# Two-layer streaming encoder on one core: where the RWKV outputs of a pair of heads stand in PE's order, and the shape of the sample's output product

## The chip, the cores and the metric

The kernel runs on one core of a Trainium2 chip. The metric is the device time of one launch in microseconds. In what follows PE is TensorE (the matrix engine), ACT is ScalarE, VectorE is also shown as DVE, POOL is GpSimd and SP is the engine that issues the DMAs.

## The reference, cut to what matters

The model takes 512 prompt rows and 32 sample rows of width 1024 through two layers. Layer 0 is RWKV-7 time mixing over 24 heads of width 64, with memory attention and a gate; layer 1 is differential attention. The change concerns layer 0's recurrence:

```
def step(S, inp):
    r_t, k_t, v_t, w_t, kk_t, a_t = inp
    sa = jnp.einsum('bhvk,bhk->bhv', S, -kk_t)
    S = (S * w_t[:, :, None, :] + sa[..., None] * (kk_t * a_t)[:, :, None, :]
         + v_t[..., None] * k_t[:, :, None, :])
    return S, jnp.einsum('bhvk,bhk->bhv', S, r_t)
...
S_T, y = lax.scan(step, S0.astype(f32), xs)
```

The kernel doesn't run this row by row. It takes 64 rows as a chunk, and computes within the chunk with matrix products.

## The kernel before, in words

**Pairs and chunks.** The 24 heads go in 12 pairs; two heads of 64 fill the 128 partitions. A pair has 8 prompt chunks, one after the other since each needs the state of the one before, and one sample chunk (index 8) with a state of its own.

**A chunk** (`chunk`) has three steps. First `ps_c<-SB,zr` multiplies by the state, and VectorE adds the result to the values (`avz`). Then `ps_c<-avz,at` solves within the chunk, and ACT copies the result into the values' rows (`sv`). Then `ps_c<-sv,bt` gives the new state, which VectorE scales and adds (`SB`). For the sample the same tiles are called `ssi`, `ats`, `svs`, `bts`.

**Values and outputs.** `rw_values` makes the parts of the values that don't need the state: 16 products of 64x64 with 64 rows (`ps_v<-sv,at`, tile form 64\*64), copied by ACT to `avz`; the larger part of them, 14, is done in one step. `rw_outputs` multiplies the finished chunks by `at` for the output rows: 16 products of 64 columns with 128 rows (`ps_yc<-sv,at`, form 128\*64), added to `yt` by VectorE; its second step transposes the pair's final state and sends it out (`ps_so`). The sample's outputs are two such products (`ps_c<-svs,ats`), one for each head, made inside `chunk` with c == 8. In the profile an fp32 product counts as two PE instructions, so 16 products are a row with x32.

**Fills.** The projections (input columns for later pairs, gates, queries) are a stream of 128x272 products, `ps_g<-hh,whi`, `hl,whi`, `hh,wlo`, cut into single PE instructions, 192 for a pair that has four blocks. They are the bulk of PE's work, and they also fill the time in which a chunk waits for VectorE or ACT. I call one of them a fill. Their weights are split into a high and a low half by ACT (`whi`) and VectorE (`wlo`); this and the finishing of a projection (`raw`, `shc`, `rkv` on ACT, `rkv` on VectorE) is put off and taken up at free places by `some`.

**What sets the order.** Each engine's order is the order in which the program is written out; the five queues are tied. In a pair's loop over the 23 steps of `PLAN`, each step runs one step of the chain (`go("chain", pr)`), then the side work that the table names, first half and second half, then fills. A row's entries are (kind, distance of the pair, PE microseconds, VectorE microseconds). The sum of the PE numbers and the fills gives the pair's whole time; each step has a share of it (`due`), and gets fills until that share is used up:

```
while left and t + MAIN / 2 < (due[k + 1] if half else (due[k] + due[k + 1]) / 2):
    next(main)
    t += MAIN
    left -= 1
```

Side work that fills its step's share thus leaves no fills there. `prep` (a generator, `rw_prep`) prepares a later pair, `val` makes values, `smp` steps the sample, `out` makes outputs, `fin` normalises them, `mrg` joins parts of an inversion that POOL runs. `MPLAN` places the steps of the memory attention in pairs 10 and 11. After pair 11, `go("out", 11)` takes the next step of its outputs, and `TAIL` has one more `out`.

In a pair's second step, `prep` needs one of the projections finished: `r = rkv["r"]()`, and `decayed` makes `zr` from it on VectorE.

Of the kernel before, what the change touches and what calls it, by code (L numbers as in the profile page):

```python
# [14 lines left out]
ALU = mybir.AluOpType  # L15
# [30 lines left out]
LATER = 0.75  # L46
FULL = ("full", 0, 0, 0)
PLAN = [
    [[("val", 0, 0.95, 0), ("prep", 2, 0.1, 0)], [("prep", 2, 0, 0.42)]],
    [[], [("prep", 2, 0, 1.04)]],  # L50
    [[("prep", 1, 0.53, 0)], [("prep", 1, 0, 0), ("prep", 2, 0.56, 1.0)]],
    [[("prep", 2, 0, 0)], [("prep", 2, 0, 1.0)]],
# [3 lines left out]
    [[("prep", 2, 1.1, 1.37)], []],  # L56
    [[("smp", 0, 0.21, 0)], [("prep", 2, 0, 0.9)]],
    [[("prep", 2, 1.1, 1.37)], [("back", 1, 0, 0)]],
    [[("smp", 0, 0.6, 0.85)], []],
    [[("prep", 2, 0.5, 0.58)], [("at", 1, 0, 0), ("fin", -1, 0, 1.0)]],  # L60
    [[("prep", 2, 0.36, 0.43)], [("inv", 2, 0, 0), ("fin", -1, 0, 0.84)]],
    [[("prep", 2, 0.36, 0.43)], [("fin", -1, 0, 0), ("prep", 3, 0, 0)]],
# [5 lines left out]
    [[("prep", 3, 0.33, 0)], [("prep", 3, 0, 0.1), ("fin", -1, 0.6, 1.0)]],  # L68
    [[("prep", 3, 0.33, 0)], [("mrg", 1, 0.9, 0), ("prep", 3, 0.33, 0), ("fin", -1, 0, 0.73)]],
    [[("prep", 3, 0, 1.45), ("val", 1, 0.45, 0)], [("prep", 3, 0, 0.5)]],  # L70
    [[("out", 0, 1.6, 0.7)], [("prep", 3, 0, 0)]]]
MEMPE = 4.8
SHIFTED, KEPT = 13, 24
LAM = 5
# [2 lines left out]
MPLAN = {10: [(0, 0), (2, 0), (3, 0), (4, 0), (5, 0), (6, 0), (6.5, 1), (7, 0), (8, 0), (9, 0), (10, 0), (11, 0), (11.5, 0), (12.5, 1),  # L77
# [3 lines left out]

FILL0 = [4, 4, 8, 2, 6, 2, 2, 2, 6, 2, 18, 4, 4, 2, 2, 0, 8, 12, 4, 8, 14, 10, 6, 14, 2, 0, 2, 2, 2, 2, 2, 2]
FILL1 = [6, 14, 12, 2, 4, 2, 2, 2, 8, 0, 10, 0, 2, 8, 8, 6, 4, 6, 6, 8, 18, 12, 8, 10, 0, 0, 0, 0, 4]
# [24 lines left out]
class Trunk:  # L108
# [796 lines left out]
    H = [slice(0, 64), slice(64, P)]  # L905
# [33 lines left out]
    def chunk(self, st, c, S, Snew):  # L939

        nc, H, yt = self.nc, self.H, st["yt"]
        e, zs, ro, A, cv, cb = self.place(st, c)
        i = c // 2
        yield
        ps = self.psc.tile([P, 4, P], F32, tag="c", name="ps_c")
        rhs = self.avz[:, e, i, :]
        sd = None
        if c:
            self.te.matmul(ps[:, 0, :], st["zr"][:, c * P : c * P + P], S[:], start=True, stop=True)
            self.ve.tensor_tensor(rhs[zs], ps[zs, 0, :], rhs[zs], ALU.add)  # L950
            yield

        self.te.matmul(ps[:, 1, :], A[0].rearrange("p h t -> p (h t)"), rhs, start=True, stop=True)
        for h in range(2):
            self.ae.copy(cv[zs, H[h]], ps[H[h], 1, H[h]])
        if c:
            self.ae.copy(yt[ro, i, :], ps[ro, 0, :])
            sd = self.rb2.tile([P, P], F32, tag="sd", name="sd", bufs=RB)
            self.ae.activation(sd[:], S[:], AF.Copy, scale=st["dl"][:, c : c + 1])
        yield  # L960
        self.te.matmul(ps[:, 2, :], cb, cv, start=True, stop=True)
        if c == 8:
            self.outputs(st, (c,), ps, 3)
        for hc in H:
            d = st["dl"][hc, c : c + 1]
            if c == 0:
                self.ve.tensor_scalar(Snew[hc, hc], ps[hc, 2, hc], d, None, ALU.mult)
            else:
                self.ve.scalar_tensor_tensor(Snew[hc, hc], ps[hc, 2, hc], d, sd[hc, hc], ALU.mult, ALU.add)
        if c == 8:  # L970
            self.ve.tensor_tensor(yt[:64, 4, :], ps[:64, 3, :], yt[:64, 4, :], ALU.add)

    def rw_chain(self, st):

# [1254 lines left out]
```

## Time and profile before

| | |
|---|---|
| runs, median (all) | 1404.84 us (1404.56, 1404.84, 1409.58) |
| profiled execution | 1403.86 us, span 1401.70 us, granted clock 0.996 |
| PE busy | 1366.8 us, 98% |
| VectorE busy | 932.2 us, 67% |
| ACT busy | 825.4 us, 59% |
| POOL busy | 376.2 us, 27% |
| layer 0's pairs | from about 132 to 690 us, 46 us for each of pairs 1 to 8 |

Rows of the timeline give the start, the duration, the engine, the operation with its tiles, and in brackets the idle time before it with what ended it. PE's ends overlap, so its rows are read by their starts. L105 is the line of the helper through which all engines' instructions go.

### The profile page before, as it was taken

Reading aid. Unit: us, or ns where it says so; the run is one execution under the profiler, and the core shown is the slowest. Engines: PE = TensorE matmul, PEld = TensorE weight load, DVE = VectorE, ACT = ScalarE, POOL = GpSimd, SP = SyncE. Lnnn points to the kernel's source line nnn. Section 1 sums busy time; section 2 is a strip of 40 time slices with the busy share of each in tenths; the row PEclk is TensorE's granted clock in tenths of the full one; section 3 lists DMA queues with packets and bytes.
Section 4 is the critical chain, followed back from the end, with each engine's and each line's share of the span. In section 5 each row is a group of like instructions: output and inputs, shape, how many; then the busy total and the mean of one; then the engine's idle time right before and its main releaser. Section 6 shows DMA issues by size and latency. Waiting matters only on the chain.

```text
span 1401.7 us, 31899 instructions
## 1 busy us (share of the span) xinstructions
PE 1366.8 (98%) x11881; PEld 1304.5 (93%) x11881; DVE 932.2 (67%) x2345; ACT 825.4 (59%) x2292; POOL 376.2 (27%) x840
## 2 busy tenths in 40 slices
PE   8999999999999999999999999999999999999997
PEld 6998899999999998898899999999999999999997
DVE  5676777787877787666753476666467756767443
ACT  5765677767776777565543366664466546665222
POOL 2136568555865586520000040000000001001100
PEclk9999999999999999999999999999999999999999
DMA  7543222332233223342364474333333322332321
GB/s 224 155 119 83 61 54 64 84 86 71 69 81 97 61 64 82 81 136 71 114 201 125 124 211 114 92 91 87 107 92 92 104 75 84 94 107 86 91 76 72
DMA packets 264036, 139.45 MB, mean 99 GB/s; under 512 B 57721, under 2 KB 252802, under 8 KB 263882
## 3 DMA queue, kind: packets, MB, share of 16 engines
q1 hardware_dynamic: 263818, 137.41, 34.9%
q8 instruction: 94, 1.54, 0.5%
q14 instruction: 60, 0.49, 0.1%
q10 hardware_dynamic: 64, 0.02, 0.0%
HBM read 111.12 MB, written 22.91 MB: 96 GB/s over the span
## 4 chain that ended last, share of the span: by engine, by line
PE 83%; DVE 8%; ACT 4%; DMA 2%; issue 2%; SPq 1%; DVEq 0%; ACTq 0%
PE ps_g L105 58%; PE ps_c L105 5%; PE ps_s L105 2%; PE ps_o L105 2%; PE ps_at L105 2%; DVE wlo L105 2%; PE ps_v L105 1%; PE ps_mo L105 1%; SPq L105 1%; PE ps_mm L105 1%; PE ps_aT L105 1%; PE ps_w L105 1%; PE ps_yc L105 1%; PE ps_ss L105 1%; PE ps_kv L105 1%
## 5 line engine op out<-in xcount | busy, mean ns | idle before, releaser
L105 PE MATMUL ps_g<-hh,wlo 128*128 128x272 f32 x1808 | 537.8, 298 | 2.4 <-DVE wlo L105 2.4
L105 PE MATMUL ps_g<-hh,whi 128*128 128x272 f32 x1808 | 538.3, 298 | 0.4 <-DVE memk L105 0.2
L105 PE MATMUL ps_g<-hl,whi 128*128 128x272 f32 x1808 | 531.9, 295 | 0.6 <-DVE hl L105 0.3
L105 PEld LDWEIGHTS ps_g<-hh,wlo 128*128 128x128 f32 x1808 | 340.9, 189 | 7.9 <-DVE wlo L105 3.5
L105 PEld LDWEIGHTS ps_g<-hh,whi 128*128 128x128 f32 x1808 | 341.7, 189 | 5.1 <-DVE og L105 0.6
L105 PEld LDWEIGHTS ps_g<-hl,whi 128*128 128x128 f32 x1808 | 341.4, 189 | 4.6 <-DVE hl L105 1.2
L105 DVE TENSOR_TENSOR wlo<-raw,whi 128x512 fp32r<-128x512 f32 x314 | 220.0, 712 | 116.8 <-ACT whi L105 112.9
L105 ACT CAST whi<-raw 128x512 fp32r<-128x512 f32 x314 | 188.8, 618 | 108.4 <-PE ps_g L105 61.3
L853 POOL TENSOR_TENSOR tm<-u,m 102x84 f32<-102x84 f32 (+23 forms) x341 | 147.9, 434 | 165.5 <-DMA m<-sc 139.7
L855 POOL TENSOR_TENSOR u<-u,tm 102x84 f32<-102x84 f32 (+23 forms) x341 | 148.9, 437 | 26.7
L105 PE MATMUL ps_g<-hi,whi 128*128 128x272 f32 x512 | 148.9, 291 | 0.0
L105 PE MATMUL ps_g<-hi,wlo 128*128 128x272 f32 x512 | 147.7, 288 | 0.5 <-DVE wlo L105 0.5
L105 PE MATMUL ps_g<-lo,whi 128*128 128x272 f32 x512 | 147.4, 288 | 0.0
L1325 POOL TENSOR_TENSOR lo<-og,hi 128x544 fp32r<-128x544 f32 x8 | 13.2, 1652 | 359.5 <-ACT hi L105 359.1
L105 PEld LDWEIGHTS ps_g<-hi,wlo 128*128 128x128 f32 x512 | 96.4, 188 | 0.7 <-DVE wlo L105 0.7
L105 PEld LDWEIGHTS ps_g<-hi,whi 128*128 128x128 f32 x512 | 96.5, 188 | 0.0
L105 PEld LDWEIGHTS ps_g<-lo,whi 128*128 128x128 f32 x512 | 96.5, 188 | 0.0
L105 DVE SCALAR_TENSOR_TENSOR SB<-ps_c,dl,sd 64x64 f32<-64x64 f32 x168 | 47.5, 283 | 43.6 <-PE ps_c L105 37.2
L105 ACT ACTIVATE pt<-ps_s,snm 128x128 f32<-128x128 f32 (+3 forms) x96 | 50.9, 531 | 41.7 <-DVE snm L105 41.6
L1746 POOL TENSOR_TENSOR hl<-hn,hh 128x544 fp32r<-128x544 f32 x8 | 12.4, 1564 | 209.8 <-ACT hh L105 209.7
L105 ACT COPY sv<-ps_c 64x64 f32<-64x64 f32 x192 | 39.3, 205 | 44.3 <-PE ps_c L105 42.6
L105 ACT ACTIVATE sg<-ps_g 128x272 f32<-128x272 f32 x64 | 25.3, 395 | 56.1 <-PE ps_g L105 51.6
(399 smaller groups left out, 2586.8 us busy)
## 6 DMA issues: line engine op xcount, KB each, us to landing
raw<-in_rw_in_dram SPq DMA_DIRECT2D x114, 256.0 KB
raw<-in_df_in_dram SPq DMA_DIRECT2D x112, 256.0 KB
raw<-in_w_out_dram SPq DMA_DIRECT2D x64, 256.0 KB
oscr<-sg SPq DMA_DIRECT2D x16, 272.0 KB
lo<-oscr SPq DMA_DIRECT2D x16, 272.0 KB
m<-sc SPq DMA_DIRECT2D x33, 128.0 KB
raw<-in_w_mem_v_dram SPq DMA_DIRECT2D x16, 256.0 KB
kh<-kh SPq DMA_DIRECT2D x24, 136.0 KB
```

The source lines that it names most:

```text
L105: return lambda *a, **k: self.trunk.tie(self, issue(*a, **k))
L853: nc.gpsimd.tensor_tensor(tm[:, :n, :wd], u3[:, :n, kx : kx + 1].to_broadcast(sh), m3[:, kx : kx + 1, kx + 1 :].to_broadcast(sh), ALU.mult)
L855: nc.gpsimd.tensor_tensor(u3[:, :n, kx + 1 :], u3[:, :n, kx + 1 :], tm[:, :n, :wd], ALU.add)
L1325: (self.nc.gpsimd if g % 2 and self.o1 else self.ve).tensor_tensor(lo[:], t, hi[:].bitcast(F32), ALU.subtract)
L1746: nc.gpsimd.tensor_tensor(self.hl[:, k, :], h[:], self.hh[:, k, :].bitcast(F32), ALU.subtract)
```

## The change: what it does

The outputs of a pair move from the last step of its own loop to the first step of the next pair's loop, directly ahead of the large step of that pair's values. Their PE number becomes 1.1 instead of 1.6. The sample's outputs become one product of the whole 128x128 array, of which the two 64x64 diagonal blocks are used, each added to `yt` by an instruction of its own; the sample's PE number there becomes 0.44 instead of 0.6. In `MPLAN`, the steps of head 3 in pair 11 move back by one place from the second on.

```
 PLAN = [
-    [[("val", 0, 0.95, 0), ("prep", 2, 0.1, 0)], [("prep", 2, 0, 0.42)]],
+    [[("out", -1, 1.1, 0.6), ("val", 0, 0.95, 0), ("prep", 2, 0.1, 0)], [("prep", 2, 0, 0.42)]],
...
-    [[("smp", 0, 0.6, 0.85)], []],
+    [[("smp", 0, 0.44, 0.95)], []],
...
-    [[("out", 0, 1.6, 0.7)], [("prep", 3, 0, 0)]]]
+    [[], [("prep", 3, 0, 0)]]]
...
-              (11, 3), (12, 3), (13, 3), (14, 3), (15, 3), (16, 3), (17, 3), (18, 3), (19, 3)]}
+              (12.5, 3), (13, 3), (14, 3), (15, 3), (16, 3), (17, 3), (18, 3), (19, 3), (20, 3)]}
...
         if c == 8:
-            self.outputs(st, (c,), ps, 3)
+            self.te.matmul(ps[:, 3, :], A[1].rearrange("p h t -> p (h t)"), cv, start=True, stop=True)
...
         if c == 8:
-            self.ve.tensor_tensor(yt[:64, 4, :], ps[:64, 3, :], yt[:64, 4, :], ALU.add)
+            for hc in H:
+                self.ve.tensor_tensor(yt[:64, 4, hc], ps[hc, 3, hc], yt[:64, 4, hc], ALU.add)
```

How the instructions stand now. First PE at the boundary between pairs 5 and 6. `ps_yc` are pair 5's outputs, `ps_v` with a number pair 6's values, the first `ps_c<-sv,bt` is the last product of pair 5's chain and `ps_c<-avz` the first of pair 6's. Before:

```order
L105 MATMUL ps_g<-hl,whi 128x272
L105 MATMUL ps_c<-sv,bt 128x128
L105 MATMUL ps_yc<-sv,at_1686 64x64 x16
L105 MATMUL ps_g<-hh,wlo 128x272
L105 MATMUL ps_c<-avz,at_89 128x128
L105 MATMUL ps_v_6352<-sv,at_89 64x64
L105 MATMUL ps_v_6353<-sv,at_89 64x64
```

And now:

```order
L105 MATMUL ps_g<-hl,whi 128x272
L105 MATMUL ps_g<-hh,wlo 128x272
L105 MATMUL ps_c<-avz,at_89 128x128
L105 MATMUL ps_yc<-sv,at_1686 64x64 x16
L105 MATMUL ps_v_6352<-sv,at_89 64x64
L105 MATMUL ps_v_6353<-sv,at_89 64x64
```

The outputs have moved behind the first product of the next chain, next to the values; 13 fills, of which the last two are shown, now stand between `ps_c<-sv,bt` and `ps_c<-avz`, where there was one.

Next the same place a little later, from the last two values on. `ps_rt` is a transpose of the preparation, `ps_c<-sv,bt` the state product of pair 6's first chunk, `ps_c<-SB` the first of its second chunk. Before:

```order
L105 MATMUL ps_v_6352<-sv,at_89 64x64 x2
L105 MATMUL ps_rt<-ident,rr 128x128
L105 MATMUL ps_g<-hh,whi 128x272
L105 MATMUL ps_g<-hl,whi 128x272
L105 MATMUL ps_g<-hh,wlo 128x272
L105 MATMUL ps_g<-hh,whi 128x272
L105 MATMUL ps_g<-hl,whi 128x272
L105 MATMUL ps_c<-sv,bt 128x128
L105 MATMUL ps_g<-hh,wlo 128x272
```

And now:

```order
L105 MATMUL ps_v_6352<-sv,at_89 64x64 x2
L105 MATMUL ps_rt<-ident,rr 128x128
L105 MATMUL ps_c<-sv,bt 128x128
L105 MATMUL ps_g<-hh,whi 128x272
L105 MATMUL ps_g<-hl,whi 128x272
```

The five fills between the values and `ps_c<-sv,bt` are gone. Up to the next `ps_c<-avz` PE now has 9, 2 and 3 fills between `ps_c<-sv,bt`, `ps_c<-SB`, `ps_b` and `ps_c<-avz`, where it had 14, 1 and 3. The boundaries into pairs 2 to 8 read alike; into pair 9 the counts are 0, 1, 0, 1 where they were 1, 10, 0, 1.

VectorE at the same boundary, from the state of pair 6's first chunk (`SB`) on; `rkv` and `zr` belong to the preparation of a later pair, `avz` is what pair 6's chain waits for. Before:

```order
L105 TENSOR_SCALAR SB_537<-ps_c,dl 64x64 x2
L105 SCALAR_TENSOR_TENSOR rkv<-raw_486,PA,rkv 128x544
L105 TENSOR_TENSOR zr_1679<-rkv,de 128x4x2x64
L105 TENSOR_TENSOR zr_1679<-rkv,de 128x32
L105 TENSOR_TENSOR avz<-ps_c,avz 64x128
L105 TENSOR_TENSOR wlo<-raw,whi 128x512
L105 SCALAR_TENSOR_TENSOR nk<-rkv,dv,ps_b 128x512
```

And now:

```order
L105 TENSOR_SCALAR SB_537<-ps_c,dl 64x64 x2
L105 SCALAR_TENSOR_TENSOR rkv<-raw_486,PA,rkv 128x544
L105 TENSOR_TENSOR zr_1679<-rkv,de 128x4x2x64
L105 TENSOR_TENSOR zr_1679<-rkv,de 128x32
L105 TENSOR_TENSOR avz<-ps_c,avz 64x128
L105 SCALAR_TENSOR_TENSOR nk<-rkv,dv,ps_b 128x512
```

Up to `avz` nothing moved; one `wlo` went from behind `avz` to a later place. ACT's order from the copies of the values to the finishing of the projection (`avz` twice, `r`, `shc`, `rkv`, `raw`) is the same before and now at this boundary; at the one into pair 1, `shc`, `rkv` and `raw` stood ahead of the copies of the values and stand behind them now.

## The prediction

> **What bounds the kernel now.** I read the busy times first, then the chain of work that ended last, then what the matrix engine (PE) waited for, and then the timeline of one pair of heads.
>
> ```profile
> PE 1366.8 (98%) x11881; PEld 1304.5 (93%) x11881; DVE 932.2 (67%) x2345; ACT 825.4 (59%) x2292; POOL 376.2 (27%) x840
> ...
> PE 83%; DVE 8%; ACT 4%; DMA 2%; issue 2%; SPq 1%; DVEq 0%; ACTq 0%
> ```
>
> PE is the bound, so PE time removed is time gained, unless PE reaches a wait earlier by it. Of PE's waits over the whole run one row matters here:
>
> ```profile
> PE ps_c L105 <- DVE avz L105: 1.9, 2, 1.4
> ```
>
> That is PE's wait for the values of the next chunk (`ps_c<-avz` behind VectorE's `avz`): 1.9 us in two places, the longest 1.4. Stretches of pair 1 and pair 7, the first and last of seven alike (length, then busy time of PE, weight load, VectorE, ACT and POOL, then PE's clock), have PE busy for all but half a microsecond of 46, at full clock:
>
> ```profile
> 223.00:269.00 46.00, 45.53 (x467) 42.83 (x466) 36.22 (x90) 33.10 (x96) 30.16 (x66) 1.00 0.29 76
> ...
> 500.00:546.00 46.00, 45.69 (x469) 42.99 (x467) 36.01 (x90) 33.25 (x96) 29.43 (x65) 1.00 0.28 73
> ```
>
> **Sample outputs (a gain).** PE's timeline, in pair 5: start, duration, operation; a row with x4 is four instructions, two for each fp32 product.
>
> ```profile
> 421.37 0.38 PE L105 MATMUL ps_c<-avz,at 128*128 128x128 f32 x2
> 421.59 0.39 PE L105 MATMUL ps_c<-ssi,zr 128*128 128x128 f32 x2
> 421.73 0.37 PE L105 MATMUL ps_g<-hh,wlo 128*128 128x272 f32 x1
> 421.94 0.29 PE L105 MATMUL ps_g<-hh,whi 128*128 128x272 f32 x1
> ...
> 429.62 0.39 PE L105 MATMUL ps_c<-svs,bts 128*128 128x128 f32 x2
> 429.93 0.45 PE L105 MATMUL ps_c<-svs,ats 128*64 128x64 f32 x4
> 430.31 0.39 PE L105 MATMUL ps_g<-hh,wlo 128*128 128x272 f32 x1
> 430.54 0.29 PE L105 MATMUL ps_g<-hh,whi 128*128 128x272 f32 x1
> ...
> 431.30 0.29 PE L105 MATMUL ps_g<-hh,whi 128*128 128x272 f32 x1
> ```
>
> Starts tell the cost, since ends overlap. A fill (`ps_g`) takes (431.30 - 430.54) / 6 = 0.127 us. From the product before the sample outputs to the second fill behind them are 0.92 us (429.62 to 430.54). With whole-array products it would be 0.22 (421.37 to 421.59, one product followed by another) plus 0.35 (421.59 to 421.94, a product and one fill): 0.57. That saves 0.35 us in each of 12 pairs: **-4.2 us**. The wait of these products is unchanged: they already stand behind `ps_c<-svs,bts`, which reads the same copy. On VectorE one add of 64x128 becomes two of 64x64:
>
> ```profile
> L105 DVE TENSOR_TENSOR yt<-ps_c,yt x12: 282/283/284, 155.0 to 663.3; 64x128 f32<-64x128 f32 x12
> ```
>
> Half the columns can't take longer than 0.28, so this adds at most 0.28 x 12 = 3.4 us to an engine with a third of its time free, and the next reader of `yt` comes many steps later; I cost it at nothing. If that cover were gone, 0.28 would stand in front of one chain step per pair.
>
> **Outputs in front of values (a small gain).** The boundary between pairs 5 and 6, all engines:
>
> ```profile
> 408.02 1.15 PE L105 MATMUL ps_yc<-sv,at 128*64 128x64 f32 x32
> 409.10 0.40 PE L105 MATMUL ps_g<-hh,wlo 128*128 128x272 f32 x1
> 409.22 0.69 DVE L105 TENSOR_TENSOR yt<-ps_yc,yt 128x512 f32<-128x512 f32 x1 [0.44 <-PE ps_yc L105]
> 409.33 0.39 PE L105 MATMUL ps_c<-avz,at 128*128 128x128 f32 x2
> 409.65 1.14 PE L105 MATMUL ps_v<-sv,at 64*64 64x64 f32 x28
> 410.72 0.33 PE L105 MATMUL ps_rt<-ident,rr 128*128 128x128 f32 x1
> 410.83 1.08 ACT L105 COPY avz<-ps_v 64x512 f32<-64x512 f32 x2 [0.28 <-PE ps_v L105]
> 411.93 0.27 ACT L105 CAST r<-ps_rt 128x128 fp32r<-128x128 f32 x1
> 412.19 0.75 ACT L105 ACTIVATE rkv<-raw,dv 128x544 f32<-128x544 f32 x1
> 412.97 0.19 ACT L105 COPY raw<-PC 128x1 f32<-128x1 f32 x1
> 413.20 0.82 DVE L105 SCALAR_TENSOR_TENSOR rkv<-raw,PA,rkv 128x544 f32<-128x544 f32 x1 [0.67 <-ACT raw L105]
> 413.94 1.11 DVE L105 TENSOR_TENSOR zr<-rkv,de 128x512 f32<-128x512 f32 x2
> 415.08 0.28 DVE L105 TENSOR_TENSOR avz<-ps_c,avz 64x128 f32<-64x128 f32 x1
> 415.42 0.38 PE L105 MATMUL ps_c<-avz,at 128*128 128x128 f32 x1
> ```
>
> Leaving the outputs' form costs the next fill 0.23 instead of 0.127 us (409.10 to 409.33), and entering the values' form makes the product ahead 0.32 instead of 0.22 (409.33 to 409.65). With the two sets adjacent both extras fall away, 0.20 us, and one change from 128\*64 to 64\*64 remains. No row shows that one directly; the nearest change between two small forms is in layer 1:
>
> ```profile
> 947.27 0.43 PE L105 MATMUL ps_os<-cv,aTs 128*32 128x128 f32 x8
> 947.62 0.42 PE L105 MATMUL ps_os<-vs,aTs 32*32 32x128 f32 x8
> 947.97 0.39 PE L105 MATMUL ps_g<-hh,wlo 128*128 128x272 f32 x1
> ```
>
> Eight products take 0.35 whether another small form or the whole array follows, so going from small to small costs what leaving does, and I keep it. If it were free, 0.13 more would be saved: 0.35 less two rounds of 0.11, half of the 0.22 above. So 0.20 to 0.33 each, taken as 0.20, at the 11 boundaries: **-2.2 us**. [...] The outputs' own add (0.69) ends before the values do (409.91 against 410.72), so `ps_rt`, which takes over its PSUM buffer, won't wait for it in the new order either.
>
> **The fills that move (the loss).** Outputs and values now stand in one step of the planner, which has no room left for fills there. In the order, PE has 23 fills between the values and the next `ps_c<-avz` before (5 + 14 + 1 + 3, between rt, sv,bt, SB, ident and b), and 14 after (0 + 9 + 2 + 3); the others now stand ahead of the outputs. That stretch isn't set by PE alone. The rows show a chain without a gap over 0.05 us, which starts when the values end: ACT's `avz` copies, `r`, `rkv` and `raw`, then VectorE's `rkv`, `zr` and `avz`, and PE takes its product at 415.42, 0.06 us after `avz` ended. It is 4.70 us long (410.72 to 415.42). Both queues keep this order after the change, so the chain keeps its length, while PE arrives 9 fills, 1.14 us, sooner, and waits. Fills that lay under the chain are run elsewhere, where PE is busy anyway. The seven boundaries into pairs 2 to 8 read alike in the order: 7 x 1.14 = **+8.0 us**. The bounds: 0, if the chain gave way, and +8.0, since no more fills leave.
>
> ```profile
> 179.64 0.33 PE L105 MATMUL ps_rt<-ident,rr 128*128 128x128 f32 x1
> ...
> 184.68 0.38 PE L105 MATMUL ps_c<-avz,at 128*128 128x128 f32 x2
> ...
> 548.83 0.33 PE L105 MATMUL ps_rt<-ident,rr 128*128 128x128 f32 x1
> ...
> 553.36 0.67 DVE L105 TENSOR_TENSOR wlo<-raw,whi 128x512 fp32r<-128x512 f32 x1
> 553.49 0.49 PE L105 MATMUL ps_c<-avz,at 128*128 128x128 f32 x2 [1.39 <-DVE avz L105]
> ```
>
> Into pair 1 the stretch is 5.04 us today, because the `rkv` part of the chain ran ahead of the values there; the new order puts it behind them. So 4.70 with 14 fills replaces 5.04 with 23: 1.14 - 0.34 = **+0.8**. Into pair 9 PE already waits 1.39; 12 fills become 2, which is 10 x 0.127 = 1.27, but one `wlo` (0.67) leaves VectorE's queue in the following stretch, where VectorE sets the pace: **+0.6**. Into pairs 10 and 11 only the `avz` copies (1.08) have to be ready, and over 2 us of PE work cover them: 0.
>
> **The last pair's memory attention (a small gain).** Head 3's steps move back in the planner's table, so two products that waited get fills ahead of them:
>
> ```profile
> 666.28 1.13 PE L105 MATMUL ps_mm<-mhk,mq 128*128 128x256 f32 x4 [0.41 <-DVE sg L105]
> ...
> 676.92 0.70 PE L105 MATMUL ps_mm<-cmk,mq 128*128 128x256 f32 x2 [0.39 <-ACT so L105]
> ```
>
> **-0.8 us** (bounds 0 and, with as much again at their neighbours, -1.6). The last pair's outputs stay alone, and its state goes out later (same instructions, one DMA, with some 90 fills still behind it): 0. The other fills shift by one here and there; eight boundaries at a fill or two each give the sum about 2 us either way.
>
> **Sum.** 8.0 + 0.8 + 0.6 - 4.2 - 2.2 - 0.8 = +2.2 us. The profiled execution took 1403.86 us (span 1401.70), which gives 1406.1; the median of the runs is 0.98 above it, so 1404.84 + 2.2 = **1407.0 us**. A difference under 0.5% (7.0 us) is about what a measurement can't tell from no change.
>
> **The rivals.**
> - *The wait doesn't grow* (0.13). ACT or VectorE catch up because PE does outputs and values without other demands on them. For it: the waits name this wait in only two places today. Against it: the chain starts from the values' end, not from a backlog. Then only gains stay: 1404.84 - 7.2 = 1397.6, or 1396.2 with a free small change; faster by 0.5%.
> - *The small-to-small change is free* (0.12), the wait grows: 1405.6.
> - *Late low halves of weights* (0.09), the slower side. VectorE's second `wlo` of the boundary stands behind `zr` now. If a block's third product then waits for it as one does at the end of layer 0 (0.79 us, below), at 8 boundaries, 6.3 us more: 1413.3. It decides from 0.6 each on. Against it: a pair of 46 us has four blocks, so a block lasts some 11 us, and `wlo` slips by about one `zr`, 1.1.
> - *The whole-array product is dearer* (0.02): if two 64-column products ran side by side, they would take 0.11 and the whole-array one 0.22, so 12 x 0.11 = +1.3 instead of -4.2: 1412.5. The rows say no (0.92 against 0.57), since both write the same half of the rows and queue up. [...]
>
> ```profile
> 690.55 0.39 PE L105 MATMUL ps_g<-hh,wlo 128*128 128x272 f32 x1 [0.79 <-DVE wlo L105]
> ```
>
> **Chances and range.** The forecast has 0.64; its own range is 1403 to 1411, from the 2 us of the shifts, the bounds of the small terms, and a microsecond or two for the spread of the runs shown (1404.56 to 1409.58). Faster by over 0.5% needs the first rival nearly whole: 0.09. Slower by over 0.5% needs the third or the fourth: 0.09. The rest, 0.82, is within 0.5%. Leaving out the outer half of the first and third rival, the range is 1399 to 1412.
>
> **What would show it.** In the profile after, `ps_c<-avz` behind the values of pairs 1 to 8 shows an idle time of about 1.1 us put down to `avz` on VectorE, and the sum of that wait goes from 1.9 to 10 or 11 us. The stretch from `ps_rt` to it stays at 4.7. `ps_yc` to `ps_v` starts 1.08 later, as to a fill. The sample's stretch reads 0.57. If the wait stays under 3 us, the loss is wrong and the first rival holds; if a row of `ps_g` behind `wlo` grows by over 4 us, the third does.

## The result, and the profile after

The changed kernel takes 1417.86 us (median of 1415.98, 1416.95, 1418.77 and 1420.81) against 1405.24 for the kernel before beside it: a ratio of 1.0091, 95% interval 1.0076 to 1.0106. It is slower by 12.6 us, where 1407.0 was forecast and 1412 was the upper end of the range. The execution shown below took 1415.98 us (span 1414.0), 12.1 more than the one shown of before.

The page of the changed kernel: busy times, and the engines' shares of the chain that ended last.

```profile
PE 1365.6 (97%) x11857; PEld 1304.4 (92%) x11857; DVE 931.2 (66%) x2357; ACT 822.4 (58%) x2292; POOL 377.6 (27%) x840
...
PE 77%; DVE 10%; ACT 7%; issue 2%; DMA 2%; SPq 1%; DVEq 0%; ACTq 0%
```

PE's busy time is 1.2 us lower in a span 12.3 us longer, and its share of the last chain fell from 83% to 77%, which VectorE and ACT took over. So the loss is waiting. Of PE's waits (sum, times, longest):

```profile
PE ps_c L105 <- DVE avz L105: 13.0, 12, 1.8
PE ps_g L105 <- DVE wlo L105: 3.6, 7, 0.9
```

The first is the predicted wait: 1.9 before, 10 to 11 forecast, 13.0 now. The second was the place of the rival with the late low halves; its limit was 4 us of growth, and it grew by 0.3. Two stretches of 46 us, one in pair 2 and one across the end of pair 5 and most of pair 6, in the columns of the table of before:

```profile
226.00:272.00 46.00, 44.26 (x437) 41.45 (x432) 36.09 (x91) 31.76 (x91) 29.89 (x66) 1.00 0.28 70
...
411.00:457.00 46.00, 44.62 (x432) 41.81 (x430) 34.78 (x88) 32.26 (x95) 28.07 (x61) 1.00 0.30 77
```

PE is idle for 1.4 to 1.7 us of 46 at full clock, where it was idle for 0.3 to 0.5. The boundary into pair 5 in the timeline:

```profile
367.07 1.15 PE L105 MATMUL ps_yc<-sv,at 128*64 128x64 f32 x32
368.15 1.14 PE L105 MATMUL ps_v<-sv,at 64*64 64x64 f32 x28
369.22 0.33 PE L105 MATMUL ps_rt<-ident,rr 128*128 128x128 f32 x1
369.33 1.08 ACT L105 COPY avz<-ps_v 64x512 f32<-64x512 f32 x2 [1.36 <-PE ps_v L105]
371.69 0.79 DVE L105 SCALAR_TENSOR_TENSOR rkv<-raw,PA,rkv 128x544 f32<-128x544 f32 x1 [1.30 <-ACT raw L105]
372.39 1.08 DVE L105 TENSOR_TENSOR zr<-rkv,de 128x512 f32<-128x512 f32 x2
373.51 0.28 DVE L105 TENSOR_TENSOR avz<-ps_c,avz 64x128 f32<-64x128 f32 x1
373.84 0.49 PE L105 MATMUL ps_c<-avz,at 128*128 128x128 f32 x2 [1.10 <-DVE avz L105]
```

Outputs and values start 1.08 apart, as foreseen. The chain from `ps_rt` to `ps_c<-avz` is 4.62 us (4.70 before), and PE waits 1.10 at its end (1.14 foreseen). Next the sample's products of the same pair:

```profile
388.88 0.39 PE L105 MATMUL ps_c<-svs,bts 128*128 128x128 f32 x2
389.10 0.39 PE L105 MATMUL ps_c<-svs,ats 128*128 128x128 f32 x2
...
389.45 0.29 PE L105 MATMUL ps_g<-hl,whi 128*128 128x272 f32 x1
```

From `ps_c<-svs,bts` to the second fill are 0.57 us (389.45 - 388.88), the number forecast, against 0.92 before.

So the large terms of the sum came true, and yet 10 us are missing from it. To see where, I matched PE's instructions other than fills between the two traces and took the difference of their starts, less 0.126 us for every fill by which the two differ up to there. Put down to places, each of pairs 3 to 8 lost 1.0 to 2.1 us, 1.6 on average, where the prediction's terms make 0.6. The three highest hold something beside the rows below: pair 5 has 0.8 in front of one more `avz`, and pairs 7 and 8 have 0.9 and 1.0 in a half-clock stretch.

| place, per pair | measured | predicted |
|---|---|---|
| boundary wait (`ps_c<-avz` behind the values) | +1.05 to +1.27 | +1.14 |
| sample outputs | -0.35 | -0.35 |
| outputs beside values | -0.22 | -0.20 |
| `ps_so` and `ps_ss`, in the later half of the pair | +0.47 | 0 |
| last chunks (`ps_c<-sv,bt` with c = 7, and after) | +0.24, given back in part | 0 |

The open question was the fourth and fifth row, and beside them the clock, which the rows on the hardware below show at half speed for 3.4 us here and there.

### The profile page after: what moved, and what is told of

Its sections match the earlier page's. It is cut to its first block, busy times and chain, and to the rows that moved or that the text cites. A ratio compares the mean times of both kernels' runs of the same rounds, so it can differ in the third digit from the quotient of the medians.

```text
span 1414.0 us, 31865 instructions
## 1 busy us (share of the span) xinstructions
PE 1365.6 (97%) x11857; PEld 1304.4 (92%) x11857; DVE 931.2 (66%) x2357; ACT 822.4 (58%) x2292; POOL 377.6 (27%) x840
## 4 chain that ended last, share of the span: by engine, by line
PE 77%; DVE 10%; ACT 7%; issue 2%; DMA 2%; SPq 1%; DVEq 0%; ACTq 0%
PE ps_g L105 54%; PE ps_c L105 4%; PE ps_s L105 2%; PE ps_at L105 2%; PE ps_o L105 2%; DVE wlo L105 1%; PE ps_v L105 1%; PE ps_w L105 1%; PE ps_mo L105 1%; PE ps_mm L105 1%; PE ps_aT L105 1%; PE ps_yc L105 1%; PE ps_ss L105 1%; SPq L105 1%; DVE at L105 1%
## 5 line engine op out<-in xcount | busy, mean ns | idle before, releaser
L853 POOL TENSOR_TENSOR tm<-u,m 102x84 f32<-102x84 f32 (+23 forms) x341 | 154.8, 454 | 174.8 <-DMA m<-sc 149.1
L855 POOL TENSOR_TENSOR u<-u,tm 102x84 f32<-102x84 f32 (+23 forms) x341 | 141.1, 414 | 26.7
L105 ACT COPY raw<-ps_g 128x272 f32<-128x272 f32 x74 | 28.3, 384 | 44.2 <-PE ps_g L105 43.9
```

The lines of the kernel that those rows point to most:

```text
L105: return lambda *a, **k: self.trunk.tie(self, issue(*a, **k))
L853: nc.gpsimd.tensor_tensor(tm[:, :n, :wd], u3[:, :n, kx : kx + 1].to_broadcast(sh), m3[:, kx : kx + 1, kx + 1 :].to_broadcast(sh), ALU.mult)
L855: nc.gpsimd.tensor_tensor(u3[:, :n, kx + 1 :], u3[:, :n, kx + 1 :], tm[:, :n, :wd], ALU.add)
```

## The experiments

Thirteen kernels were run. Three accounts were in play: the boundary wait of the prediction; the place of put-off work in the queues of ACT and VectorE, which moves when the fills shift; and half-clock stretches of PE.

### The sample's product alone, and the outputs alone

The first kernel is the kernel before with the two edits in `chunk` and no number of the planner changed:

```
-            self.outputs(st, (c,), ps, 3)
+            self.te.matmul(ps[:, 3, :], A[1].rearrange("p h t -> p (h t)"), cv, start=True, stop=True)
...
-            self.ve.tensor_tensor(yt[:64, 4, :], ps[:64, 3, :], yt[:64, 4, :], ALU.add)
+            for hc in H:
+                self.ve.tensor_tensor(yt[:64, 4, hc], ps[hc, 3, hc], yt[:64, 4, hc], ALU.add)
```

> The kernel before with the sample's outputs as one whole-array product (and the two adds), all numbers of the table unchanged, so that every other instruction stands where it stood. Term of the sum, by both theories: 0.35 us less in each of 12 pairs, -4.2 us, to 1400.6. If the two half adds were on VectorE's path, up to 0.28 x 12 = 3.4 of it would be given back (1404). If the whole-array product saved nothing, 1404.8.

Measured: 1404.05 (1402.37 to 1405.66), ratio 0.9991 (0.9982 to 1.0000); some 0.5 us gained of 4.2, hardly clear of noise. The stretch itself is 0.35 shorter in every pair. VectorE's halves of the add, by form (minimum, median and maximum in ns):

```profile
L105 DVE TENSOR_TENSOR yt<-ps_c,yt x24: 216/221/226, 154.8 to 664.2; 64x64 f32<-64x64 f32 x24
```

Two halves take 0.44, the one add took 0.28. At the next `ps_c<-avz`, whose `avz` is behind them on VectorE, 0.08 to 0.19 us of each pair's 0.35 came back. The rest went with two half-clock stretches, at 214 and 490 us, in pairs that lost about 0.9 where their neighbours gained 0.3.

The second kernel has the other part alone: outputs moved, with the new row of `PLAN[0]`, the empty last row and the new `MPLAN`; the sample as before.

> The changed kernel with the sample's outputs as before (two products, one add, numbers 0.6 and 0.85): the outputs are moved alone. If the loss lies in the move, as the theory of the boundary wait and that of the put-off work both say, it is the changed kernel plus 4.2: about 1422, within 2 us since the sample's numbers move a fill here and there. If the loss beyond the forecast came with the sample's change (its adds, its numbers), this one is at the forecast's 1407 + 4 = 1411 or under.

Measured: 1422.83 (1418.97 to 1423.22), ratio 1.0123 (1.0109 to 1.0137), as expected: the loss is in the moved outputs, together with the new numbers that this kernel gives them in the planner.

### Is it the boundary wait?

The third kernel is the changed kernel with the step that makes `zr` (and needs `rkv`) moved from `PLAN[1]` to behind the boundary's `avz`:

```
-    [[], [("prep", 2, 0, 1.04)]],
-    [[("prep", 1, 0.53, 0)], [("prep", 1, 0, 0), ("prep", 2, 0.56, 1.0)]],
+    [[], []],
+    [[("prep", 1, 0.53, 0)], [("prep", 2, 0, 1.04), ("prep", 1, 0, 0), ("prep", 2, 0.56, 1.0)]],
```

> The changed kernel with the preparation step that makes zr taken one step later, behind the chain's avz on VectorE; PE's order in pairs 1 to 8 is the same. Theory of the boundary wait: zr (1.11 us) leaves the way of avz, so PE's wait of 1.4 to 1.6 us behind the values falls to 0.3 to 0.5 in 8 or 9 pairs: -8 to -10 us, about 1409, and the waits of the later steps stay. Rival, that the wait is set by something behind zr or by ACT's queue: at most -3, 1415 or more.

Measured: 1417.32 (1415.77 to 1418.08), ratio 1.0086. Its waits:

```profile
PE ps_q L105 <- POOL rkk L773: 6.1, 7, 1.3
...
PE ps_c L105 <- DVE avz L105: 3.0, 8, 0.8
```

The wait is gone (13.0 to 3.0), and the time is not: what was put later is missed a step later, as 6.1 us at `ps_q` shows. The boundary wait explains the rows, but its removal bought nothing here. That it alone makes the loss is refuted.

The fifth kernel takes it away otherwise, by giving the outputs no numbers in the planner, so that the stretch gets 22 fills again:

```
-    [[("out", -1, 1.1, 0.6), ("val", 0, 0.95, 0), ("prep", 2, 0.1, 0)], [("prep", 2, 0, 0.42)]],
+    [[("out", -1, 0, 0), ("val", 0, 0.95, 0), ("prep", 2, 0.1, 0)], [("prep", 2, 0, 0.42)]],
```

> The changed kernel with the outputs at their new place, but their numbers there set to 0, so that the planner leaves fills between the values and the next chain product: 22 between the values and the second ps_c<-avz (5, 12, 1, 4), where the changed kernel has 14 and the one before 23; in exchange every fourth step or so has one fill less. Theory of the fills that left: the boundary wait is back at 0.3 us, -1.1 in 8 pairs, and with the outputs beside the values and the sample product kept, about 1408 (1405 to 1410). Rival, that the pair is held by its chain through VectorE and ACT and a wait that is taken away here comes back at the next step, as with zr later: 1415 or more.

Measured: 1417.19 (1414.10 to 1420.37), ratio 1.0089. Against before, the place costs 0.1 in place of 1.2, while `ps_so` costs 0.31, `ps_ss` 0.28 and the last chunk's `ps_c<-sv,bt` 0.12 per pair. Again about the same total.

### Is it the place of the put-off work?

The eighth kernel changes no instruction: the kernel before, with only the new numbers in its planner, the outputs at their old place.

```
-    [[("smp", 0, 0.6, 0.85)], []],
+    [[("smp", 0, 0.44, 0.95)], []],
...
-    [[("out", 0, 1.6, 0.7)], [("prep", 3, 0, 0)]]]
+    [[("out", 0, 1.1, 0.6)], [("prep", 3, 0, 0)]]]
```

> The kernel before with the changed numbers alone (outputs 1.1 and 0.6, still at their old place; sample 0.44 and 0.95); no instruction is changed, and fills shift by one at some steps (the outputs are followed by 4 fills instead of 1). If a shift of a fill here and there costs 0.5 us in a pair, this is 1409; if the shift matters only where put-off work changes its place, which it hardly does here, 1405 within 1.

Measured: 1412.45 (1410.81 to 1413.17), ratio 1.0049 (1.0035 to 1.0063). Fills that stand elsewhere by a few cost 7.3 us, without a product moved or added. Neither expected time came; what the second of them left out is shown behind the next kernel.

The ninth changes less: two fills of pair 0 go to pair 8 (`each[pr]` is the number of fills that a pair gets), so between them the stream of fills is late by two.

```
+            each[0] += -2
+            each[8] -= -2
```

> The kernel before with pair 0 taking 2 fills fewer and pair 8 as many more, and nothing else: in pairs 1 to 7 every count of fills between two other PE instructions is as before, only the stream of projections stands 2 fills later, so that the last fill of one half comes behind ps_c<-sv,bt and ps_q instead of ahead of them. Theory of the crossing: ACT's copy of that half (raw<-ps_g) stands in ACT's queue ahead of gsq, uh, sq, bv, bts and svs and waits for this fill, 0.9 us later than before; PE then waits 0.2 us at ps_so and 0.2 at ps_ss and at the next steps: 0.3 to 0.6 us a pair in 7 pairs, 1407 to 1410. Rival, that what counts is how many fills cover each step: 1405, since these counts are unchanged.

Measured: 1410.22 (1409.08 to 1413.25), ratio 1.0035 (1.0022 to 1.0048): two fills later, +4.9 us. A projection's half is 24 fills. When its last fill is done, ACT can copy it out (`raw<-ps_g`), and what follows in ACT's queue is behind that copy. Before, pair 6 (PE and ACT; `raw` is named with its wait for the last fill):

```profile
435.34 0.30 PE L105 MATMUL ps_g<-hh,wlo 128*128 128x272 f32 x1
435.47 0.39 PE L105 MATMUL ps_c<-sv,bt 128*128 128x128 f32 x2
435.67 0.39 ACT L105 COPY raw<-ps_g 128x272 f32<-128x272 f32 x1 [0.73 <-PE ps_g L105]
435.69 0.62 PE L105 MATMUL ps_q<-rkk,hb 128*128 128x272 f32 x2
435.95 0.74 ACT L105 ACTIVATE gsq<-yt 128x640 f32<-128x640 f32 x1
438.96 0.26 ACT L105 COPY svs<-ps_bts 32x128 f32<-32x128 f32 x1
439.48 0.38 PE L105 MATMUL ps_c<-avz,at 128*128 128x128 f32 x2
440.14 0.27 PE L105 MATMUL ps_so<-ident,SS 128*128 128x128 f32 x1
```

And with the stream two fills late:

```profile
441.30 0.38 PE L105 MATMUL ps_c<-sv,bt 128*128 128x128 f32 x2
441.52 0.62 PE L105 MATMUL ps_q<-rkk,hb 128*128 128x272 f32 x2
442.11 0.28 PE L105 MATMUL ps_g<-hh,wlo 128*128 128x272 f32 x1
442.43 0.39 ACT L105 COPY raw<-ps_g 128x272 f32<-128x272 f32 x1 [1.65 <-PE ps_g L105]
442.71 0.74 ACT L105 ACTIVATE gsq<-yt 128x640 f32<-128x640 f32 x1
445.29 0.38 PE L105 MATMUL ps_c<-avz,at 128*128 128x128 f32 x2
445.72 0.26 ACT L105 COPY svs<-ps_bts 32x128 f32<-32x128 f32 x1
446.03 0.14 PEld L105 LDWEIGHTS ps_so<-ident,SS 128*128 128x128 f32 x1 [0.16 <-ACT svs L105]
```

Before, the half's last fill (435.34) stands in front of `ps_c<-sv,bt`, and `raw` starts 0.20 after that product. With two fills more the last one falls behind `ps_c<-sv,bt` and `ps_q`, and `raw` starts 1.13 after the product. The rest of ACT's queue is late by the same amount: `svs` was copied before `ps_c<-avz`, and now after it, and PE's weight load for `ps_so` waits for it. In pairs 2, 3, 4, 6 and 7 it is 0.3 to 0.5 us each. Of the run shown, 3.5 us more were lost in pair 0 and 2.4 in pair 5. Both hold a half-clock stretch that the kernel before doesn't have (6.83 us from 134.45, 3.41 us from 404.11), and pair 5 a wait of 1.0 for `avz`. So the crossing itself is seen in some 2 us of the loss, and the rest of the 4.9 isn't shown to be its work.

The eighth kernel has the same crossing. In its pairs 1 to 8 the half's last fill stands one fill behind `ps_q`, and `raw` waits for it as in the ninth; in pair 6:

```profile
442.56 0.39 ACT L105 COPY raw<-ps_g 128x272 f32<-128x272 f32 x1 [1.65 <-PE ps_g L105]
```

So put-off work did change its place there, which the expectation held it hardly would.

In the changed kernel the same wait comes by another queue: VectorE takes up put-off `wlo` and `sg` ahead of the `yt` that ACT's `gsq` needs.

```profile
394.47 0.43 DVE L105 SCALAR_TENSOR_TENSOR sg<-sg,ps_g 128x272 f32<-128x272 f32 x1
394.82 0.82 DVE L105 TENSOR_TENSOR yt<-yt,gs 128x640 f32<-128x640 f32 x1
395.67 0.74 ACT L105 ACTIVATE gsq<-yt 128x640 f32<-128x640 f32 x1 [1.19 <-DVE yt L105]
398.96 0.26 ACT L105 COPY svs<-ps_bts 32x128 f32<-32x128 f32 x1
399.27 0.14 PEld L105 LDWEIGHTS ps_so<-ident,SS 128*128 128x128 f32 x1 [0.33 <-ACT svs L105]
```

If this is the cause, a shift the other way must help the changed kernel. The first attempt (the fourth kernel), seven fills earlier with VectorE's numbers as before:

```
-    [[("out", -1, 1.1, 0.6), ...
+    [[("out", -1, 1.1, 0), ...
-    [[("smp", 0, 0.44, 0.95)], []],
+    [[("smp", 0, 0.44, 0.85)], []],
-    [[], [("prep", 3, 0, 0)]]]
+    [[("full", 0, 0, 0.7)], [("prep", 3, 0, 0)]]]
...
+            each[0] += 7
+            each[8] -= 7
```

> The changed kernel with the put-off work (finishing of projections, low halves) brought back to the places on VectorE and ACT that it had before: pair 0 takes 7 fills more and pair 8 as many less, and the outputs' and the sample's VectorE numbers are counted as before. PE's counts of fills between its other instructions are the same in pairs 1 to 7. Theory of the put-off work: the three or four small waits on ACT in a pair (0.23 to 0.26 us each, ps_so, ps_ss, ps_c<-sv,bt) and the second avz wait go, 0.5 to 0.7 us a pair: -4 to -6, 1412 to 1414, while the boundary wait of 1.4 stays. Rival, that these waits come from the fills' new places on PE: no change, 1418.

Measured: 1420.56 (1417.94 to 1420.71), ratio 1.0109: worse by 2.7, a miss. Seven was the wrong number: the half's end came to stand just behind `ps_q` (three fills, then seven), and five half-clock stretches fell into the run. The tenth kernel is the same with 10 in place of 7, which puts the end ahead of `ps_c<-sv,bt`.

> The changed kernel with the stream of projections 10 fills ahead (pair 0 takes 10 more, pair 8 as many less) and the VectorE numbers of the outputs and the sample as before, so that the halves end at the same chain steps as in the kernel before and VectorE and ACT have nearly its order; fills between PE's other instructions are as in the changed kernel. Theory of the crossing: the waits at ps_so, ps_ss and ps_c<-sv,bt (0.5 to 0.7 us a pair) go, and VectorE's rkv ahead of SB shortens the chain behind the values by some 0.8: -8 to -10 us, 1408 to 1410. Rival, that the waits follow the counts of fills: 1417 to 1420, as with 7 fills.

Measured: 1407.09 (1403.49 to 1410.18), ratio 1.0010 (1.0001 to 1.0018). The same instructions as in the changed kernel take 10.8 us less. From the fourth kernel it differs by three fills alone, and by 13.5 us: there `raw` waits 1.81 us for a last fill behind `ps_q`, here 0.73 for one ahead of `ps_c<-sv,bt`, and PE's wait for `avz` falls from 11.7 to 3.5 us over the run. Up to pair 7 it gains 3.6 us on the kernel before, and it loses 8 from pair 8 to the end of layer 0, where the ten fills are given back and where half-clock stretches stand at 551.36 (3.41 us) and 636.70 (6.83 us). So the twelfth kernel gives them back in pair 11:

```
-            each[8] -= 10
+            each[11] -= 10
```

> As the aligned kernel (stream 10 fills ahead, VectorE numbers as before), but the 10 fills are given back in pair 11 instead of pair 8, so that pairs 8 to 10 stay aligned too. In the aligned run the stretch up to pair 7 gained 3.7 us on the kernel before, and pairs 8 to 11 lost 8.5. Theory of the crossing: that loss is the alignment given up in pair 8 and two or three half-clock windows; most of it goes, 1400 to 1403, faster than the kernel before. Rival, that pairs 9 to 11 lose by the outputs' move itself: 1405 to 1407.

Measured: 1402.43 (1401.16 to 1406.89) against 1405.08, ratio 0.9987 (0.9978 to 0.9996): the whole change is in it, it is 15.4 us below the changed kernel and faster than the kernel before. Up to the boundary into pair 9 its trace is 4.1 us ahead of the kernel before, which is most of what the sample's product and the neighbouring outputs and values were forecast to gain up to there (0.55 in each of nine pairs, 5.0). Its boundary into pair 5:

```profile
363.27 1.14 PE L105 MATMUL ps_v<-sv,at 64*64 64x64 f32 x28
364.14 0.83 DVE L105 SCALAR_TENSOR_TENSOR rkv<-raw,PA,rkv 128x544 f32<-128x544 f32 x1
364.35 0.33 PE L105 MATMUL ps_rt<-ident,rr 128*128 128x128 f32 x1
364.45 1.08 ACT L105 COPY avz<-ps_v 64x512 f32<-64x512 f32 x2 [0.39 <-PE ps_v L105]
365.55 0.99 DVE L105 TENSOR_TENSOR zr<-rkv,de 128x512 f32<-128x512 f32 x2
367.18 0.28 DVE L105 TENSOR_TENSOR avz<-ps_c,avz 64x128 f32<-64x128 f32 x1
367.71 0.38 PE L105 MATMUL ps_c<-avz,at 128*128 128x128 f32 x2
```

ACT's `raw` and `rkv` had been done before the values ended, so VectorE's `rkv` starts at 364.14, while PE still makes the values, and not at the end of the chain. The stretch from `ps_rt` to `ps_c<-avz` is 3.36 us in place of 4.62, and the wait is gone with the same 14 fills in it. The wait of the prediction was itself a matter of where the put-off work stood. Over the run:

```profile
PE ps_c L105 <- DVE avz L105: 1.6, 3, 0.7
```

The eleventh kernel joined the outputs without numbers (fifth kernel) with a shift of six:

```
+    [[("out", -1, 0, 0), ("val", 0, 0.95, 0), ("prep", 2, 0.1, 0)], [("prep", 2, 0, 0.42)]],
...
+            each[0] += 6
+            each[8] -= 6
```

> The changed kernel with the outputs' numbers at 0 (22 fills stay in the stretch behind the values) and the stream 6 fills ahead, so that the half in question ends ahead of ps_c<-sv,bt and ps_q again. If the boundary wait and the crossing are the whole loss, the small waits (0.8 to 1.0 us a pair in the run without the shift) go as well: 1402 to 1407, with the gains of the sample and of the adjacency left. If a wait that is taken away always comes back at another step, 1415 or more.

Measured: 1421.10 (1420.45 to 1421.49), ratio 1.0110: a miss by over 14 us. The put-off `rkv` landed on VectorE between `avz` and `bk` (in the kernel before it stands behind `bk`), and these waits came:

```profile
PE ps_at L105 <- DVE bk L105: 6.9, 10, 1.0
PE ps_c L105 <- DVE avz L105: 5.5, 15, 1.6
...
PE ps_y L105 <- DVE yt L105: 4.5, 11, 0.6
```

A shift does good only if all of the put-off work lands well; one place was foreseen by counting, the other not.

### Is it the clock?

Half-clock stretches (shown below) fell behind the short products `ps_ss` and `ps_w`. Three kernels put 10 fills in place of 5 between them, by two numbers, in the sample kernel, in the changed kernel and in the twelfth:

```
-    [[("prep", 3, 1.04, 0.17)], [("mrg", 1, 0, 0.86)]],
-    [[("mrg", 1, 0.9, 0)], [("rsq", 0, 0, 1.5)]],
+    [[("prep", 3, 0.3, 0.17)], [("mrg", 1, 0, 0.86)]],
+    [[("mrg", 1, 0.7, 0)], [("rsq", 0, 0, 1.5)]],
```

> The kernel before with the whole-array sample product, and PE numbers of two steps lowered (1.04 to 0.3, 0.9 to 0.7), so that 10 fills instead of 5 stand between ps_ss (10 instructions of 2 columns) and ps_w (32 of 32 rows and 32 columns). Theory of the clock: with the sample product alone two windows of 3.41 us ran at half clock, each right behind a stretch that held all of ps_ss and ps_w, and cost about 1.2 us each; with fills between them none does, the granted clock is 0.996 as before, and the time is 2 to 3 us under the sample product alone, 1401 to 1402. Rival, that the half-clock windows come by chance or from something else, or cost nothing: 1404.

> The changed kernel with the same two PE numbers lowered: 10 fills instead of 5 between ps_ss and ps_w. Theory of the clock: the changed kernel's runs have clocks of 0.988 to 0.995 against 0.995 to 0.996 before, which is 1 to 7 windows of 3.41 us at half clock more; without them 3 to 4 us of the median go, 1414, and the runs lie closer together. Rival, that the clock is not set by this stretch: 1418 as it was, with the same spread.

> The same with 10 fills instead of 5 between ps_ss and ps_w (PE numbers 0.3 and 0.7). Theory of the clock: fewer half-clock windows, 1 to 2 us under the kernel without it, unless the lower numbers shift the halves' ends again by a fill or two, which by the theory of the crossing could cost as much: 1399 to 1405.

Measured: 1403.39 (ratio 0.9987, 0.9978 to 0.9996), 1415.85 (1.0076, 1.0063 to 1.0089) and 1403.88 (0.9990, 0.9980 to 1.0001). In all three profiles no half-clock stretch is left in pairs 1 to 7 (before these pairs, and at 577 to 606 us, some remain); the twelfth kernel has none there without the edit either. Against the same kernels without the edit that is -0.7, -2.0 and +1.5 us. All three intervals overlap those without the edit, so none of these differences is clear of noise, and the seventh kernel's runs (1413.05 to 1418.63) lie no closer together than those of the changed kernel.

What the clock took is better read otherwise. The changed kernel's run at 0.995, a clock that the kernel before has too, took 1415.98, still 10.7 us above the median of before; its runs at 0.988 to 0.993 took 1.0 to 4.8 us more. So the clock has a part of the 12.6, some 2 us by this estimate, and most of the loss isn't the clock.

## Why the prediction was wrong, point by point

- **Boundary wait: right in size, incomplete in cause.** +1.05 to +1.27 a pair (1.14), chain of 4.62 (4.70). Its first rival, that it wouldn't grow, is false for the kernel as given. But it was taken as a fixed price of the moved outputs, since "both queues keep this order after the change"; the twelfth kernel shows 14 fills and no wait. (The prediction's rows at 421 to 431 us are pair 6's, and its stretches at 223 and 500 us pair 2's and pair 8's; the numbers read from them hold.)
- **Sample outputs: right on PE** (0.57, as forecast). The extra add "at nothing" was wrong for the product alone: 0.44 in place of 0.28, of which 0.08 to 0.19 a pair reached PE in the first kernel, about 1 to 2 us in all. In the changed kernel the place keeps its 0.35. The cover named, that the next reader of `yt` is far, was the wrong cover: what stands behind the add on VectorE is the chain's `avz`.
- **Outputs beside values: right** (0.22 against 0.20). The change from 128\*64 to 64\*64 isn't free: 1.08 from outputs to values, as to a fill, so the second rival falls.
- **Late low halves** didn't come (+0.3 us over the run), nor did the **dearer whole-array product** (0.57 against 0.92 at the sample); the prediction gave both a small chance. That the two products of before queue up shows in the starts in its trace: the sample's four instructions, which write one half of the rows, start at 429.93, 430.04, 430.10 and 430.16, the last three 0.06 apart, while those of `ps_yc`, of the same form and with products for both halves in turn, start in twos, 0.01 apart, and 0.06 from two to two (408.12 and 408.13, 408.18 and 408.19).
- **The small terms.** In pair 1 the boundary wait cost 1.4 against 0.8. Into pair 9 it grew from 1.39 to 1.78, 0.4 against 0.6. Both waits of the last pair's memory attention (0.41 and 0.39) are gone, 0.8 as forecast.
- **The failed step** is the sentence "The other fills shift by one here and there; eight boundaries at a fill or two each give the sum about 2 us either way". It priced a shift at the length of the fills shifted. In the runs the price follows what the shift moves past what in ACT's and VectorE's queues: in the changed kernel +3.7 us at `ps_so` and `ps_ss`; by the numbers alone +7.3; two fills late +4.9, of which some 2 are seen at the crossing; ten fills early, with VectorE's numbers as before, -10.8 and, with the return in pair 11, -15.4. The term was a range of 2 and should have been of some 10 with either sign.
- **The clock** was not in the sum at all. The kernel before ran mostly at a granted clock of 0.995 to 0.996, the changed one at 0.988 to 0.995; some 2 us, by the estimate above.

In the run shown, the matched rows of pairs 1 to 8 make a loss of 11.7 us. The boundary wait has 9.4 of it (8.8 forecast for these pairs), the sample's product -2.8 and the outputs beside the values -1.7 (-2.8 and -1.6 forecast). What the sum had at nothing is `ps_so` and `ps_ss` with 3.7, the two half-clock stretches with 1.9, and other places with 1.2. Of these, 0.8 stand in front of one `avz` of pair 5, by put-off work again: `raw` waits 1.09 us for its last fill, so VectorE's `rkv` comes at 384.19, behind `at` and with this pair's `lam` right in front of that `avz`, where it ran ahead of `SB` and `at` before. These are places, not causes: in the twelfth kernel the boundary wait went together with the small ones, while in the third and the fifth it went and others came. How much of the loss is owed to which shifted piece of put-off work isn't separable from these runs, since each shift also moves the half-clock stretches.

## What to carry to other kernels

Where a planner lays a steady stream of work between the steps of a chain, a change of its cost numbers is a change of the kernel: find in the order where the stream's own milestones (here the last fill of a half) cross the chain's products, and price each crossing by the queue that stands behind the copy that it releases, not by the fills' length. One milestone put right isn't enough, as the eleventh kernel shows. Before a change that shifts such a stream is judged, try it with the milestones put back to where they stood: here the same change is 0.9% slower or 0.1% faster. A wait that an edit removes is worth what the next step can use, and that was nothing in two kernels of three.

## What the runs showed of the hardware

PE's clock, by stretches of 3.41 us (columns as before; PE's clock is the third number from the end), in the changed kernel around 498.57 us:

```profile
491.74:495.16 3.42, 3.33 (x27) 2.98 (x25) 1.94 (x5) 3.31 (x10) 0.00 (x0) 1.00 0.78 239
495.16:498.57 3.41, 3.25 (x51) 2.90 (x51) 2.33 (x8) 0.86 (x5) 0.96 (x4) 1.00 0.18 51
498.57:501.98 3.41, 3.41 (x16) 3.41 (x17) 2.76 (x9) 3.18 (x11) 2.81 (x8) 0.50 0.54 153
501.98:505.40 3.42, 3.42 (x32) 3.22 (x32) 2.32 (x8) 2.58 (x7) 2.87 (x8) 1.00 0.08 24
```

The clock falls to 0.50 for one such stretch and comes back; 16 instructions pass in it, where 27 and 32 pass in the first and the last of these stretches, and a fill takes 0.227 us (500.72 to 501.85, five fills) in place of 0.126 (the median in pairs 1 to 8 before). It cost 0.9 and 1.0 us in pairs 7 and 8 here, and about 1.2 each time in pairs 1 and 7 of the first kernel. The stretch ahead had PE counted as busy for 3.25 of 3.41 us, but this is what ran in it:

```profile
495.34 1.28 PE L105 MATMUL ps_ss<-hsel,sq 128*128 128x2 f32 x10
497.50 1.00 PE L105 MATMUL ps_w<-t1b,at 32*32 32x32 f32 x32
```

That is products of two columns and of 32x32, with six fills and the two instructions of one state product among them. The falls start on a grid: in this trace 167.48, 498.57, 546.36 and 1409.93 us lie 97, 14 and 253 times 3.413 us apart (331.09, 47.79 and 863.57 us). 14 times is 47.79 us, near a pair's length, so whether both groups of products come to lie within one stretch of the grid changes with a microsecond's drift, and with it the clock.

The other traces bear this out. In pairs 1 to 8 of the kernels with five fills between the two groups, `ps_ss` began within 0.27 us of a stretch's start nine times (above by 0.18: 495.34 against 495.16), so that both groups lay in that stretch, and each time the next one ran at half clock. Eight more half-clock stretches came there behind one whose edge cut one of the groups; such a stretch went either way. With ten fills between (sixth, seventh and thirteenth kernel), `ps_ss` began so early four times, and the clock never fell.
